# Held weight splits moved from GpSimd to VectorE, and the second token half of a skewed GEMM ordered behind the first

## The chip, the cores and the metric

The kernel runs on one core of a Trainium2 chip. The metric is device time in microseconds (us) of one launch; less is better. Three runs of the kernel before took 1042.84, 1040.69 and 1042.12 us, with a median of 1042.12 us.

## What is computed

One decoder block on 256 tokens of width 2048, all in float32. The part that matters here is the way from the mixer's output to the output of the block:

```python
mixed = jnp.concatenate([pool_out, attn_out], axis=-1) @ w_out[l]
h = h + rms_norm(mixed, post_mix_norm[l])

hn = rms_norm(h, pre_ffn_norm[l])
ff = (jax.nn.silu(hn @ w_gate[l]) * (hn @ w_up[l])) @ w_down[l]
h = h + rms_norm(ff, post_ffn_norm[l])
```

`w_out` is 2048 x 2048, `w_gate` and `w_up` are 2048 x 5632, and `w_down` is 5632 x 2048. Ahead of it stand a normalisation, the projection to queries, keys and values, a pooling mixer and differential attention.

## The kernel before

**How a product is made.** Every float32 weight tile is split into a high part and the rest: ScalarE copies the tile into a reduced format (the high part, L99), and another engine subtracts that from the original (the low part, L100). Activations are split the same way. A product is then three matmuls that add up in one PSUM bank: activation high by weight high (L135), activation low by weight high (L136), activation high by weight low (L137). So each 128-row step of the contraction, called a k-step below, costs three matmuls for each half of the tokens. The 256 tokens are two halves of 128, called t = 0 and t = 1, and each half has its own PSUM bank. Weights come in tiles of 128 x 1024 by DMA from SyncE's queue (L83), two k-steps to a tile, and are split tile by tile in `split` (L97).

**Two ways through a GEMM.** `gemm_a` (L141) takes the k-steps in order and does both token halves at each. `gemm_a_skew` (L149) does so too, except for a run of "held" k-steps: their split weights are kept, then all held k-steps are done for t = 0, and after that all of them for t = 1. If the last k-step is a held one, the function hands out the finished bank of t = 0 as soon as its matmuls are written, so that what follows for t = 0 can run beside the matmuls of t = 1.

Skewed GEMMs are used in three places:
- The last of four column blocks of `w_out` (`closing`, called at L609) holds its last 12 k-steps. What follows for each token half is the sum of squares (ScalarE, L536), the gain (VectorE, L540), a reciprocal root of a few tiny instructions (L190 to L205) and the addition to the residual in four column blocks (VectorE, L563, tile `xn`).
- The first column block of `w_gate` (L614) holds its first 12 k-steps, that is, six weight tiles. The first three go into ring buffers, the next three into the six `hold` buffers, which the held weights of `w_out` use before them.
- The last column block of `w_down` (`closing`, L850) holds its last 8 of 44 k-steps; behind it come the same steps as behind `w_out` (tile `x` instead of `xn`), and then the stores of the result (L848).

**Between `w_out` and `w_gate`.** The new residual has to be transposed for the gate GEMM: `h_parts` (L582) transposes a block of 128 tokens by 512 columns on TensorE (four matmuls by the identity, L586), and for each of its four k-steps ScalarE makes the high part (L592) and VectorE the low part (L593). The tables `H_OUT` and `H_GATE` say behind which held k-step each of these blocks is written: three blocks of t = 0 in the midst of the `w_out` matmuls of t = 1, the fourth behind the gate's first k-step, and the blocks of t = 1 behind the gate's held k-steps of t = 0 and, for the last block, of t = 1.

**What sets the order.** The order of instructions on each engine isn't the program's order. A planner runs the program against a cost model (L906) and puts next on an engine what it thinks can run first. `tc.issue_after(ins)` restrains it: what is written inside the block is placed behind `ins` on `ins`'s engine. `behind[0]` is such an instruction for the matmuls of `mm_a` (L134): it starts as nothing, and each call of `h_parts` sets it to its last transpose (L587). Nothing else sets it, so the matmuls of t = 1 aren't bound to follow those of t = 0 on that account, and in `w_down` the last setter is a transpose of long before.

**Who splits the held weights of the gate.** L615 gives `split` its buffers and its engine: the first three tiles are ring buffers with VectorE, the next three are hold buffers with GpSimd (`pool`). Those three subtractions are the only ones of the 128 x 1024 kind that GpSimd does.

Of the kernel before, what the change touches and what calls it, by code (L numbers as in the profile page):

```python
# [29 lines left out]
H_GATE = {(0, 0): (0, 3), (0, 7): (1, 0), (0, 9): (1, 1), (0, 11): (1, 2), (1, 2): (1, 3)}  # L30
RING = 3
# [14 lines left out]
def block_kernel(ctx: ExitStack, tc: tile.TileContext, x, xT, pos, cols, rows, lamv, invf, invcnt,  # L46
                 w_in, w_u, w_pool, w_out, w_g0, w_u0, w_gu, w_down, out):
    nc = tc.nc
    mm, act, dve, pool, sync = nc.tensor, nc.scalar, nc.vector, nc.gpsimd, nc.sync
# [10 lines left out]
    def nm(s):  # L60
        uid[0] += 1
        return f"{s}_{uid[0]}"
# [4 lines left out]
    def bank():  # L67
        return psum.tile([P, 512], F32, tag="mm", name=nm("mm"), bufs=4)
# [42 lines left out]
    def a_steps(srcs, order=None, held=range(0), parts=None):  # L111

        i = 0
        for s in order or range(len(srcs)):
            raws = [load(srcs[s], half) for half in range(2)]
            for half in range(2):
                by = parts(i) if i in held else ()
                if by != "halves":
                    hi, lo = split(raws[half], *by)
                for j in range(2):  # L120
                    c = slice(j * 512, (j + 1) * 512)
                    if by == "halves":
                        w = split(raws[half][:, c], lambda: (half_tile("wh"), half_tile("wl")))
                    else:
                        w = hi[:, c], lo[:, c]
                    yield i, 4 * s + 2 * half + j, *w
                    i += 1

    behind = [None]
    before_k = [lambda c, i: None]  # L130

    def mm_a(ps, a, t, k, wh, wl, first, last):

        with tc.issue_after(behind[0]) if behind[0] is not None else nullcontext():  # L134
            mm.matmul(ps[t][:, :], lhsT=a[0](k, t), rhs=wh, start=first, stop=False)  # L135
            mm.matmul(ps[t][:, :], lhsT=a[1](k, t), rhs=wh, start=False, stop=False)  # L136
            last_mm[0] = mm.matmul(ps[t][:, :], lhsT=a[0](k, t), rhs=wl, start=False, stop=last).ins  # L137

    last_mm = [None]
# [9 lines left out]
    def gemm_a_skew(srcs, a, nk, order, held_at, parts, hook):  # L149


        ps = [bank(), bank()]
        held = []
        for i, k, wh, wl in a_steps(srcs, order, held_at, parts):
            if i in held_at:
                held.append((i, k, wh, wl))
                if len(held) < len(held_at):
                    continue
                for t in range(2):
                    for n, (i, k, wh, wl) in enumerate(held):  # L160
                        mm_a(ps, a, t, k, wh, wl, i == 0, i == nk - 1)
                        hook(t, n)
                    if i == nk - 1:
                        yield t, ps[t]
            else:
                for t in range(2):
                    mm_a(ps, a, t, k, wh, wl, i == 0, i == nk - 1)
        if nk - 1 not in held_at:
            for t in range(2):
                yield t, ps[t]  # L170
# [358 lines left out]
    def closing(srcs_of, a, nk, gains, order, tail, parts, hook, done):  # L529
# [26 lines left out]
        for t, ps in gemm_a_skew(srcs_of(3), a, nk, order, range(nk - tail, nk), parts, hook):  # L556
            square(3, t, ps[:, :])
            v = variance(sst[:, t, 3:4], 1.0 / D, pre2[:, t:t + 1])
            gained(3, t, ps[:, :])
            rs = rsqrt(v)  # L560
            for c in range(4):
                for z in (slice(0, 256), slice(256, 512)) if c == 0 and t == 1 else (slice(0, 512),):
                    dve.scalar_tensor_tensor(h_c(c, t)[:, z], mg[c, t][:, z], rs, h_c(c, t)[:, z], ALU.mult, ALU.add)  # L563
                    done(c, t, z)
# [14 lines left out]
    hold_parts = lambda: (hold.tile([P, 1024], F32R, tag=f"h{z}", name=nm(f"h{z}"), bufs=HOLD // 2) for z in ("hi", "lo"))  # L579
    rstd3 = cp.tile([P, 2], F32, name="rstd3")  # L580

    def h_parts(t, c):  # L582

        tr = bank2() if c % 2 == 0 else psum2.tile([P, 512], F32, tag="hs", name=nm("hs"), bufs=2)
        for j in range(4):
            last = mm.transpose(tr[:, j * P:(j + 1) * P], xn[t][:, (4 * c + j) * P:(4 * c + j + 1) * P], ident)  # L586
        behind[0] = last.ins  # L587
        for j in range(4):
            k = 4 * c + j
            o = tr[:, j * P:(j + 1) * P]  # L590
            hi, lo = (z(k)[:, t * P:(t + 1) * P] for z in (hh_k, hl_k))
            behind_act[0] = act.activation(hi, o, AF.Copy, scale=g3(k)).ins  # L592
            dve.scalar_tensor_tensor(lo, o, g3(k), hi.bitcast(F32), ALU.mult, ALU.subtract)  # L593
# [3 lines left out]
    def h_stats(t):  # L597
        for c in range(4):
            j2 = cp.tile([P, 512], mybir.dt.bfloat16, tag="sqj", name=nm("sqj"), bufs=2)
            with tc.issue_after(behind_act[0]):  # L600
                act.activation(j2, h_c(c, t), AF.Square, accum_out=ss3[:, t, c:c + 1])
        ss3s = small([P, 1])
        dve.tensor_reduce(ss3s, ss3[:, t, :], AX.X, ALU.add)
        dve.tensor_copy(rstd3[:, t:t + 1], rsqrt(variance(ss3s, 1.0 / D)))

    def h_hook(at):
        return lambda t, n: h_parts(*at[t, n]) if (t, n) in at else None
# [4 lines left out]
    a_h = (lambda k, t: hh_k(k)[:, t * P:(t + 1) * P], lambda k, t: hl_k(k)[:, t * P:(t + 1) * P])  # L612
    sg = []
    for t, ps in gemm_a_skew([w_g0[i] for i in range(4)], a_h, NKD, None, range(HOLD),  # L614
                             lambda i: (ring_parts, dve) if i < 2 * RING else (hold_parts, pool), h_hook(H_GATE)):  # L615
        h_stats(t)
        sg.append(cp.tile([P, 512], F32, tag="gain", name=f"sg{t}", bufs=2))
        act.activation(sg[t], ps[:, :], AF.Silu, scale=rstd3[:, t:t + 1])
# [291 lines left out]
```

## Time and profile before

| | |
|---|---|
| Median of three runs | 1042.12 us |
| The profiled execution's own time | 1042.59 us |
| Its span from first to last instruction | 1040.8 us |
| Granted TensorE clock, mean over the span | 0.997 |
| TensorE matmul busy | 1018.6 us, 98% of the span |
| VectorE busy | 733.4 us, 70% |
| ScalarE busy | 538.8 us, 52% |
| GpSimd busy | 34.6 us, 3% |
| Chain that ended last | TensorE 85%, DMA 6%, VectorE 6% |

The times of the trace are counted from the span's start. A matmul's duration in the trace is a modelled one of 0.39 us, while matmuls that nothing holds up start 0.23 us apart; so a gap is best read from start to start. "Idle before" names what ended the idle time in front of an instruction. The chain of waits follows the work that ended last, back from the last instruction, and shows at each step what released it.

The stages that matter lie at these times: the held matmuls of `w_out` from 288.66 us, the matmuls of the first gate block from 309.13 us, ten rounds of gate and up blocks from 356.18 to 789 us, `w_down` to 1030.5 us, and the last steps and stores to 1040.8 us.

### The profile page before, as it was taken

What the parts mean: (1) busy time and instruction counts of PE and PEld (TensorE: products, weight loads), DVE (VectorE), ACT (ScalarE), POOL (GpSimd) and SP (SyncE); (2) the same over time, 40 slices, a digit from 0 to 9 for tenths busy, and PEclk for the clock granted to TensorE, in tenths of its full rate; (3) what the DMA queues carried; (4) which work ended last, traced back from release to release, by engine and by line L of the source; (5) the groups of instructions that cost most, each with busy time, mean ns of one, the idle gap of its engine ahead of it and who ended that gap; (6) DMA issues with size and microseconds to landing.
All of it is one profiled execution on the core that took longest, in us unless ns stands there. A gap on an engine that the chain in (4) does not pass through costs nothing.

```text
span 1040.8 us, 12565 instructions
## 1 busy us (share of the span) xinstructions
PE 1018.6 (98%) x4787; PEld 839.4 (81%) x4787; DVE 733.4 (70%) x847; ACT 538.8 (52%) x643; POOL 34.6 (3%) x57
## 2 busy tenths in 40 slices
PE   8999999999999999999999999999999999999996
PEld 5788888988877788888878878878888888888884
DVE  6648755875677978889798887888877664454444
ACT  6746545664547655454554545545555653343431
POOL 0003200210030000000000000000000000000000
PEclk9999999999999999999999999999999999999998
DMA  8853555456754556555655556645565575556542
GB/s 321 293 182 122 178 185 166 156 168 220 245 198 158 175 207 207 180 181 207 212 191 186 177 191 211 209 167 183 199 211 202 206 286 193 194 192 212 195 169 81
DMA packets 57517, 203.39 MB, mean 195 GB/s; under 512 B 6896, under 2 KB 7792, under 8 KB 56688
## 3 DMA queue, kind: packets, MB, share of 16 engines
q1 hardware_dynamic: 57168, 202.44, 56.8%
q8 instruction: 37, 0.61, 0.2%
q14 instruction: 24, 0.20, 0.1%
q10 hardware_dynamic: 288, 0.15, 0.0%
HBM read 198.37 MB, written 4.19 MB: 195 GB/s over the span
## 4 chain that ended last, share of the span: by engine, by line
PE 85%; DMA 6%; DVE 6%; issue 1%; SPq 1%; ACT 1%; DVEq 0%; ACTq 0%
PE mm L137 15%; PE mm L136 15%; PE mm L135 15%; PE mm L757 8%; PE mm L755 7%; PE mm L756 7%; DMA raw<-in_w_gu 4%; PE tr L757 2%; PE tr L756 2%; PE tr L755 2%; DVE wl L695 2%; PE mm L173 2%; PE mm L175 2%; PE mm L174 1%; PE m L755 1%; DVE xn L563 1%
## 5 line engine op out<-in xcount | busy, mean ns | idle before, releaser
L100 DVE TENSOR_TENSOR wl<-raw,wh 128x1024 fp32r<-128x1024 f32 x88 | 104.7, 1222 | 106.9 <-ACT wh L99 106.9
L100 DVE TENSOR_TENSOR wlo<-raw,whi 128x1024 fp32r<-128x1024 f32 x97 | 119.2, 1230 | 70.3 <-ACT whi L99 64.0
L99 ACT ACTIVATE wh<-raw 128x1024 fp32r<-128x1024 f32 x88 | 89.3, 1052 | 122.0 <-PE mm L136 117.3
L99 ACT ACTIVATE whi<-raw 128x1024 fp32r<-128x1024 f32 x97 | 102.1, 1057 | 78.0 <-PE mm L136 60.7
L136 PE MATMUL mm<-wh,gl 128*128 128x512 f32 x352 | 137.1, 390 | 0.0
L695 DVE TENSOR_TENSOR wl<-raw,wh 128x2048 fp32r<-128x2048 f32 x50 | 114.4, 2287 | 31.2 <-ACT wh L702 31.2
L135 PE MATMUL mm<-wh,gh 128*128 128x512 f32 x352 | 134.8, 389 | 0.0
L137 PE MATMUL mm<-wl,gh 128*128 128x512 f32 x352 | 130.7, 389 | 0.0
L755 PE MATMUL mm<-wh,h 128*128 128x512 f32 x330 | 128.6, 390 | 0.0
L756 PE MATMUL mm<-wh,h 128*128 128x512 f32 x330 | 128.6, 390 | 0.0
L757 PE MATMUL mm<-wl,h 128*128 128x512 f32 x330 | 115.6, 394 | 3.8 <-DVE wl L695 3.8
L702 ACT ACTIVATE wh<-raw 128x2048 fp32r<-128x2048 f32 x50 | 95.5, 1910 | 44.7 <-PE tr L756 39.8
L702 ACT ACTIVATE wh<-T 128x2048 fp32r<-128x2048 f32 x30 | 57.3, 1911 | 60.4 <-DVE T L706 55.4
L695 DVE TENSOR_TENSOR wl<-T,wh 128x2048 fp32r<-128x2048 f32 x30 | 68.6, 2287 | 23.1 <-ACT wh L702 23.1
L135 PE MATMUL mm<-whi,x 128*128 128x512 f32 x192 | 75.1, 395 | 3.5 <-ACT whi L279 2.7
L137 PEld LDWEIGHTS mm<-wl,gh 128*128 128x128 f32 x352 | 66.1, 188 | 13.7
L136 PEld LDWEIGHTS mm<-wh,gl 128*128 128x128 f32 x352 | 66.0, 188 | 13.8
L757 PEld LDWEIGHTS mm<-wl,h 128*128 128x128 f32 x330 | 61.9, 188 | 18.7 <-DVE wl L695 6.1
L135 PEld LDWEIGHTS mm<-wh,gh 128*128 128x128 f32 x352 | 66.0, 188 | 13.5
L136 PE MATMUL mm<-whi,x 128*128 128x512 f32 x192 | 74.6, 391 | 0.0
L756 PEld LDWEIGHTS mm<-wh,h 128*128 128x128 f32 x330 | 61.9, 188 | 13.0
L755 PEld LDWEIGHTS mm<-wh,h 128*128 128x128 f32 x330 | 62.0, 188 | 12.6
(243 smaller groups left out, 1910.6 us busy)
## 6 DMA issues: line engine op xcount, KB each, us to landing
raw<-in_w_gu SPq DMA_DIRECT2D x160, 512.0 KB, 4.5
raw<-in_w_down SPq DMA_DIRECT2D x88, 512.0 KB, 4.1
raw<-in_w_in SPq DMA_DIRECT2D x46, 512.0 KB, 3.7
raw<-in_w_out SPq DMA_DIRECT2D x32, 512.0 KB, 4.0
raw<-in_w_u SPq DMA_DIRECT2D x24, 512.0 KB, 3.6
raw<-in_w_g SPq DMA_DIRECT2D x8, 512.0 KB, 5.9
xn<-in_x SPq DMA_DIRECT2D x2, 1024.0 KB, 9.1
gain<-in_rows SPq DMA_DIRECT2D x8, 256.0 KB, 4.9
```

Of the source, the lines that this page charges most:

```text
L99: last_split[0] = act.activation(hi, raw, AF.Copy).ins
L100: (by or dve).tensor_tensor(lo, raw, hi.bitcast(F32), ALU.subtract)
L135: mm.matmul(ps[t][:, :], lhsT=a[0](k, t), rhs=wh, start=first, stop=False)
L136: mm.matmul(ps[t][:, :], lhsT=a[1](k, t), rhs=wh, start=False, stop=False)
L137: last_mm[0] = mm.matmul(ps[t][:, :], lhsT=a[0](k, t), rhs=wl, start=False, stop=last).ins
L173: mm.matmul(o, lhsT=wh, rhs=xh, start=st, stop=False)
L175: mm.matmul(o, lhsT=wl, rhs=xh, start=False, stop=sp)
L695: last_low[0] = dve.tensor_tensor(res, x, hi.bitcast(F32), ALU.subtract).ins
L702: act.activation(res, x, AF.Copy)
L755: mm.matmul(o, lhsT=a[0], rhs=wh, start=first, stop=False)
L756: mm.matmul(o, lhsT=a[1], rhs=wh, start=False, stop=False)
L757: mm.matmul(o, lhsT=a[0], rhs=wl, start=False, stop=left[i] == 0)
```

## The change

Two edits, each of a line. In `gemm_a_skew`, after the held matmuls of a token half, `behind[0]` is set to the last of them. So the matmuls of t = 1 are placed behind all held ones of t = 0, and whatever `mm_a` writes later is placed behind the last held one of t = 1. It holds in all three skewed GEMMs. It also replaces what `h_parts` had set inside the loop. In the gate's call, the engine is taken out of the pair: all six held tiles are split by VectorE, which is the default of `split`; the buffers are the same.

```diff
@@ -160,6 +160,7 @@
                     for n, (i, k, wh, wl) in enumerate(held):
                         mm_a(ps, a, t, k, wh, wl, i == 0, i == nk - 1)
                         hook(t, n)
+                    behind[0] = last_mm[0]
                     if i == nk - 1:
                         yield t, ps[t]
             else:
@@ -612,7 +613,7 @@
     a_h = (lambda k, t: hh_k(k)[:, t * P:(t + 1) * P], lambda k, t: hl_k(k)[:, t * P:(t + 1) * P])
     sg = []
     for t, ps in gemm_a_skew([w_g0[i] for i in range(4)], a_h, NKD, None, range(HOLD),
-                             lambda i: (ring_parts, dve) if i < 2 * RING else (hold_parts, pool), h_hook(H_GATE)):
+                             lambda i: (ring_parts if i < 2 * RING else hold_parts,), h_hook(H_GATE)):
         h_stats(t)
```

## The prediction

> **What bounds the kernel now.** I read the page's header first, then the chain of waits between the end of `w_out` and the ten rounds, then the timelines of each engine there and behind the last matmul.
>
> ```profile
> span 1040.8 us, 12565 instructions
> PE 1018.6 (98%) x4787; PEld 839.4 (81%) x4787; DVE 733.4 (70%) x847; ACT 538.8 (52%) x643; POOL 34.6 (3%) x57
> ```
>
> TensorE is the bound for nearly the whole span, so a change that adds or drops no matmul can win only where TensorE stands still, or behind its last matmul. The chain shows where:
>
> ```profile
> 299.30 9.25 DVE xn L563 x4
> ...
> 314.62 2.77 DVE xn L563 x5
> ...
> 317.72 0.50 PE mm L136
> ```
>
> It runs on TensorE before this and after it. In between VectorE holds it. Four residual additions of t = 0 take 9.25 us; the same four blocks of t = 1 (five instructions, one block being halved) take 2.77. Beside the slow ones stands the only other thing that differs:
>
> ```profile
> L563 DVE SCALAR_TENSOR_TENSOR xn<-mg,tiny,xn x2: 2874/2934/2993, 299.3 to 302.2; 128x512 f32<-128x512 f32 x2
> ...
> 307.90:308.60 0.70, 0.65 (x1) 1.00 0.00 0
> L100 POOL TENSOR_TENSOR hlo<-raw,hhi x3: 2400/2836/2837, 299.3 to 304.5; 128x1024 fp32r<-128x1024 f32 x3
> ```
>
> The first row has VectorE's first two additions, of 2.99 and 2.87 us (the three times are the least, the median and the most, in ns). The second is a stretch in which only the fourth runs, for 0.65 us, so about 2.7 us are left for the third: 9.25 - 2.99 - 2.87 - 0.65. The third row has GpSimd's three splits, which begin at 299.3 and end at 304.5 + 2.84 = 307.3. So three additions each last about one GpSimd split, and the fourth, after GpSimd is done, 0.65 us. That is taking turns: each waits until the other's whole instruction is over.
>
> The Trainium skill, SBUF — State Buffer, section Who interferes with whom, states this: a VectorE instruction with both inputs in SBUF and a GpSimd instruction that reads SBUF use one port in turn, and the later one is blocked for the other's whole length. The 2.87 us beside the 0.65 us agree with it.
>
> **What the first edit is worth.** TensorE waits for these additions three times, since the transposes of `h_parts` read `xn`:
>
> ```profile
> 301.35 0.39 PE L137 MATMUL mm<-hlo,mh 128*128 128x512 f32 x1
> 302.35 0.66 PE L586 MATMUL tr<-ident,xn 128*128 128x128 f32 x4 [0.61 <-DVE xn L563]
> ...
> 304.00 0.40 PE L137 MATMUL mm<-hlo,mh 128*128 128x512 f32 x1
> 305.14 0.65 PE L586 MATMUL hs<-ident,xn 128*128 128x128 f32 x4 [0.75 <-DVE xn L563]
> ...
> 306.80 0.40 PE L137 MATMUL mm<-hlo,mh 128*128 128x512 f32 x1
> 307.94 0.66 PE L586 MATMUL tr<-ident,xn 128*128 128x128 f32 x4 [0.74 <-DVE xn L563]
> ...
> 309.58 0.39 PE L137 MATMUL mm<-wlo,h 128*128 128x512 f32 x1
> 309.81 0.60 PE L586 MATMUL hs<-ident,xn 128*128 128x128 f32 x4
> 310.17 0.48 PE L135 MATMUL mm<-whi,h 128*128 128x512 f32 x1
> ...
> 315.07 0.83 PE L586 MATMUL tr<-ident,xn 128*128 128x128 f32 x4
> 315.66 0.48 PE L135 MATMUL mm<-hhi,h 128*128 128x512 f32 x1
> ...
> 316.67 0.60 PE L586 MATMUL hs<-ident,xn 128*128 128x128 f32 x4
> 317.72 0.50 PE L136 MATMUL mm<-hhi,h 128*128 128x512 f32 x1 [0.45 <-DVE h L593]
> ```
>
> I count from start to start. A block of transposes that nobody holds up starts 0.23 us behind the matmul before it (309.58 to 309.81), and the next matmul 0.36 us after that. The three held-up ones start 1.00, 1.14 and 1.14 us behind: too late by 0.77 + 0.91 + 0.91 = 2.59 us. At 315.07 and 316.67 the next matmul comes after 0.59 and 1.05 us: too late by 0.23 + 0.69 = 0.92 us.
>
> Without GpSimd the four additions take about 2.8 us and end near 302.1. The three splits come to VectorE instead:
>
> ```profile
> L100 DVE TENSOR_TENSOR wlo<-raw,whi 128x1024 fp32r<-128x1024 f32 x97 | 119.2, 1230 | 70.3 <-ACT whi L99 64.0
> 300.87 1.06 ACT L99 ACTIVATE hhi<-raw 128x1024 fp32r<-128x1024 f32 x1 [0.30 <-PE mm L136]
> 313.70 0.39 PE L135 MATMUL mm<-hhi,h 128*128 128x512 f32 x1
> ```
>
> Three times 1.23 is 3.69 us. Even with all of them ahead of the `h` splits, VectorE comes to those at 299.3 + 2.8 + 3.7 = 305.8 rather than at 299.30 + 9.25 = 308.55, so it gains 2.7 us while it does the more work. If one split stands ahead of each addition, they end at 301.2, 303.2 and 305.1, and TensorE, unheld, asks for them at 301.6, 303.4 and 305.2: still no stall. Only if all three splits stood ahead of the first addition (the third can't start before its high part is made at 300.87 + 1.06 = 301.9) would that addition end at 301.9 + 1.23 + 0.7 = 303.9, and TensorE would wait 2.3 of its 2.6 us again. So this term is between 0.3 and 2.6; I take 2.59, since the additions are ready at 299.3 and the second and third splits aren't. The matmuls with the moved weights start at 313.70, so by 311 in the new run, and the splits are done by 306 or so: nobody waits for them. SyncE's loads wait for the raw tiles that these splits free, which comes sooner than GpSimd's 307.3.
>
> The 0.92 us hang on t = 1's additions at 314.6. Their chain starts with ScalarE's sum of squares:
>
> ```profile
> 308.90 0.39 PE L137 MATMUL mm<-hlo,mh 128*128 128x512 f32 x1
> 311.73 0.59 ACT L536 ACTIVATE sqj<-mm 128x512 bf16<-128x512 f32 x1
> ```
>
> The bank of t = 1 is ready at 308.90 + 0.39 = 309.29, but ScalarE gets to it 2.44 us later, since it is still at the `h` parts that VectorE held up. With those done sooner it can start at once, so relative to TensorE the additions come up to 2.4 us sooner, and the 0.92 us go too. Bounds: 0 (VectorE, fuller by 3.7 us, hands the delay on) and 1.2 (some matmuls up to 319.6 also start late by tenths). I take 0.92. First edit: 2.59 + 0.92 = 3.5 us, with bounds 0.3 and 3.8.
>
> Does it survive to the end? Behind 317.72 the waits view has these two rows for TensorE, and no other:
>
> ```profile
> PE mm L757 <- DVE wl L695: 3.8, 4, 1.2
> PE mm L755 <- ACT rh L702: 0.5, 1, 0.5
> ```
>
> The second is one wait at the start of the ten rounds, the first four waits in them (total, times, longest). The loads and splits that end them wait in their turn for buffers that TensorE frees, so a start that is 3.5 us sooner moves all of it. I put the passing on at no cost, with the rounds' order as a rival below.
>
> **What the second edit is worth.** In the gate the new order forbids filling t = 1's held steps with later k-steps; the `h` parts those need should come over 2 us sooner by the first edit, so I price that at zero (a stall there could cost some tenths). The other two places show in the matmuls, in ScalarE's sums of squares and in what VectorE does behind them:
>
> ```profile
> 297.07 0.60 ACT L536 ACTIVATE sqj<-mm 128x512 bf16<-128x512 f32 x1 [5.97 <-PE mm L137]
> ...
> 1019.44 0.39 PE L135 MATMUL mm<-wh,gh 128*128 128x512 f32 x1
> ...
> 1028.48 0.60 ACT L536 ACTIVATE sqj<-mm 128x512 bf16<-128x512 f32 x1 [7.06 <-PE mm L137]
> 1029.20 0.21 DVE L190 TENSOR_SCALAR tiny<-sst,tiny 128x1 f32<-128x1 f32 x1 [6.33 <-ACT sqj L536]
> 1030.10 0.39 PE L137 MATMUL mm<-wl,gh 128*128 128x512 f32 x1
> 1030.52 0.60 ACT L536 ACTIVATE sqj<-mm 128x512 bf16<-128x512 f32 x1 [0.87 <-PE mm L137]
> 1033.36 0.21 DVE L190 TENSOR_SCALAR tiny<-sst,tiny 128x1 f32<-128x1 f32 x1
> ```
>
> In `w_out` t = 0's sum starts at 297.07, 12 us ahead of the end of t = 1's bank at 309.29: the halves are in order already, and the edit is worth nothing there. In `w_down` the planner mixed them. The last matmul ends at 1030.10 + 0.39 = 1030.49. The 48 held ones start at 1019.44, so they are (1030.10 - 1019.44) / 47 = 0.227 us apart. With the halves in order, t = 0 ends 24 of them sooner, at 1025.05; now its sum of squares starts only at 1028.48. VectorE's steps for t = 0 run from 1029.20 to 1033.36, and only then does it take up t = 1, whose sum of squares started at 1030.52. In order, t = 0's 4.16 us begin at about 1025.8 and end at 1030.0, before t = 1 needs VectorE: 0.72 us behind 1030.52 (the step from 1028.48 to 1029.20), at 1031.24 instead of 1033.36. That is 2.12 us, and what follows stays as long as it is. It needs t = 0's last weights in time:
>
> ```profile
> 1019.41 2.01 ACT L99 ACTIVATE wh<-raw 128x1024 fp32r<-128x1024 f32 x2 [3.43 <-PE mm L136]
> 1020.51 2.36 DVE L100 TENSOR_TENSOR wl<-raw,wh 128x1024 fp32r<-128x1024 f32 x2 [3.08 <-ACT wh L99]
> ```
>
> In order, the fifth k-step's come 12 matmuls later, at 1022.2, the seventh's at 1023.5, each low part 0.45 us after that; the splits are done at 1021.7 and 1022.9. A margin of 0.9 us or more, so no stall. I keep 1.6 to 2.4 as bounds for small shifts.
>
> **Sum.** 3.5 + 2.1 = 5.6 us. The profiled execution's own 1042.59 becomes 1037.0; it is 0.47 above the median of 1042.12, which becomes 1036.5.
>
> **The rivals.** *The order in the rounds changes (slower).* The planner lays the program out anew, and the rounds depend on how transfers and splits fall. Four waits of 3.8 us in all, the longest 1.2, hold TensorE up in ten rounds; from start to start a wait is 0.16 us longer (0.77 against 0.61 above), so 4.4 us in all and 1.4 at most. If all ten rounds took the worst layout, that is 14 us, 9.6 more: 1036.5 + 9.6 = 1046.1. It decides against the change once more than four further rounds wait (4 x 1.4 = 5.6). For it: rounds of the same code now come out differently. Against: the planner sees about the same inputs there. The same thing the other way, no waiting round, would give 1036.5 - 4.4 = 1032.1.
>
> *VectorE becomes the bound.*
>
> ```profile
> 297.00:309.00 12.00, 9.90 (x48) 7.43 (x48) 10.87 (x11) 4.50 (x8) 8.00 (x3) 1.00 0.15 54
> 309.00:321.00 12.00, 11.55 (x58) 8.76 (x57) 9.54 (x31) 6.75 (x24) 0.00 (x0) 1.00 0.74 264
> ```
>
> The third busy figure is VectorE's: 10.87 + 9.54 = 20.4 of 24 us. If the 9.25 us of additions were real work, 3.69 more would make 24.1 and push t = 1's additions and all behind them by up to 3.7: 1042.1 + 3.7 - 2.1 = 1043.7, slower than before by less than can be told. The Trainium skill, Perfetto Trace Analysis, section Optimizing Scalar/DVE Operations, speaks for this rival: where VectorE is saturated, handing work to GpSimd may pay (it adds that the shared port may spoil it). The 0.65 us of the fourth addition says that 6.5 of the 9.25 us are waiting, so I give it little.
>
> *Only the end is gained.* The planner sets the splits ahead of the additions: 0.3 of the first edit and 2.1 of the second, 1042.1 - 2.4 = 1039.7.
>
> *The second edit does nothing,* since the planner's mixing came from elsewhere: 1042.1 - 3.5 = 1038.6. The edit forbids the mixing by name, so this is the least likely.
>
> **Chances.** Forecast 0.62 (1035.9 to 1038.0: 2.5 to 3.8 us by the first edit, 1.6 to 2.4 by the second); only the end 0.14; rounds better 0.08, rounds worse 0.08; VectorE bound 0.05; second edit void 0.03. The range runs from 1033.5 (half of the better rounds) to 1039.8. About 0.2%, 2.1 us, is what a measurement of this kernel can tell from no change: faster means below 1040.0. The forecast, most of the end-only case, the better rounds and the void edit lie there: 0.84. Slower (above 1044.2) takes most of the worse rounds: 0.06. The rest, 0.10, is the same.
>
> **What would show it.** The four additions of t = 0 should take about 0.7 us each with no GpSimd instruction beside them; the idle time ahead of the transposes that VectorE ended (0.61, 0.75, 0.74) should be gone, and the gate's first matmul should come 2.6 us sooner; t = 1's sum of squares in `w_out` should start within 0.5 us of its bank's end. At the end, t = 0's sum of squares should start 5.4 us ahead of t = 1's, and some 8.2 us, not 10.3, should lie between the last matmul and the span's end. I am wrong if the additions stay near 2.9 us, if a wait for a low part `hlo` appears, or if the rounds' length changes by over 0.5 us each.

## The result and the profile after

The changed kernel took 1055.98 us (median of four runs, 1053.40 to 1057.19); the kernel before took 1042.44 us beside it (1040.69 to 1042.84). The ratio is 1.013, with a 95% interval of 1.0114 to 1.0147: slower, where 1036.5 us had been forecast. The profiled execution took 1056.83 us. In the changed kernel every line from L164 on has a number one greater than before.

First the page's header and the shares of the chain.

```profile
span 1055.0 us, 12573 instructions
PE 1024.1 (97%) x4787; PEld 841.9 (80%) x4787; DVE 730.0 (69%) x850; ACT 539.7 (51%) x643; POOL 26.6 (3%) x54
...
PE 80%; DVE 7%; DMA 7%; issue 3%; ACT 2%; SPq 1%; DVEq 0%; ACTq 0%
```

The matmuls are as many as before. TensorE's share of the chain fell from 85 to 80%, so it stood still more. To see where, I cut each span at four marks: the first held matmul of `w_out` (`hhi` by `mh`), the first product of the rounds (`rh` by `h`), the first of `w_down` (`wh` by `gh`) and the last L135 matmul.

| us | middle | ten rounds | `w_down` | end |
|---|---|---|---|---|
| before | 67.5 | 433.3 | 240.1 | 11.1 |
| after | 65.7 | 452.1 | 240.2 | 9.0 |

Both places that the change touches became shorter, by 1.9 and 2.1 us (taken before rounding). The ten rounds, in which it changes no line, became 18.8 us longer.

**The middle,** from the timeline of the changed kernel:

```profile
299.81 2.73 DVE L564 SCALAR_TENSOR_TENSOR xn<-mg,tiny,xn 128x512 f32<-128x512 f32 x4
301.01 0.60 PE L587 MATMUL tr<-ident,xn 128*128 128x128 f32 x4
...
305.80 0.39 PE L135 MATMUL mm<-whi,h 128*128 128x512 f32 x1
...
306.06 0.60 ACT L537 ACTIVATE sqj<-mm 128x512 bf16<-128x512 f32 x1 [0.58 <-PE mm L137]
...
312.06 0.50 PE L136 MATMUL mm<-whi,h 128*128 128x512 f32 x1 [1.27 <-DVE h L594]
```

The four additions of t = 0 take 2.73 us instead of 9.25, and the transposes have no idle time noted. The gate's first matmul comes 17.7 us behind the first mark (305.80 - 288.08) instead of 20.5 (309.13 - 288.66). The sum of squares of t = 1 waits for TensorE alone. The last row is a wait of a kind that the kernel before has once, with 0.45 us (at 317.72): TensorE waits 1.27 us for a low part of `h`.

**The end,** from the timelines of TensorE, ScalarE and VectorE:

```profile
1041.43 0.60 ACT L537 ACTIVATE sqj<-mm 128x512 bf16<-128x512 f32 x1 [3.65 <-PE mm L137]
...
1046.44 0.39 PE L137 MATMUL mm<-wl,gh 128*128 128x512 f32 x1
1046.87 0.60 ACT L537 ACTIVATE sqj<-mm 128x512 bf16<-128x512 f32 x1 [4.27 <-PE mm L137]
1047.59 0.21 DVE L191 TENSOR_SCALAR tiny<-sst,tiny 128x1 f32<-128x1 f32 x1 [1.20 <-ACT sqj L537]
```

The sum of squares of t = 0 stands 5.44 us ahead of that of t = 1, VectorE takes t = 1 up 0.72 us behind it, and 8.2 us lie between the last matmul's end (1046.83) and the span's.

**The rounds.** TensorE's waits behind 318 us in the changed kernel (total, times, longest):

```profile
PE mm L756 <- ACT wh L703: 5.2, 4, 1.7
PE m L756 <- ACT gT L677: 5.0, 9, 0.7
PE mm L756 <- ACT rh L703: 3.9, 5, 1.8
PE mm L758 <- DVE wl L696: 3.5, 4, 1.3
```

Before there were 4.3 us in 5 waits; now there are 17.6 us in 22. That is 13.3 us more, and 17 more times the 0.16 us that a wait is longer from start to start, 2.7. The windows of 10 us show the rest (behind the window and its length stand the busy times of TensorE's matmuls, its weight loads, VectorE, ScalarE and GpSimd, with their instructions in brackets, then the granted clock, the DMA share and GB/s):

```profile
500.00:510.00 10.00, 7.93 (x32) 5.87 (x31) 6.46 (x6) 4.05 (x3) 0.00 (x0) 0.94 0.38 134
510.00:520.00 10.00, 10.00 (x41) 8.13 (x40) 4.99 (x3) 3.74 (x3) 0.00 (x0) 0.89 0.76 268
580.00:590.00 10.00, 6.74 (x29) 4.76 (x29) 8.22 (x8) 6.28 (x7) 0.00 (x0) 1.00 0.10 29
670.00:680.00 10.00, 7.26 (x26) 5.15 (x24) 8.07 (x8) 4.99 (x5) 0.00 (x0) 0.83 0.02 5
```

The clock is below 0.995 in three windows of the rounds, which costs at most (0.06 + 0.11 + 0.17) x 10 = 3.4 us. In all that makes 13.3 + 2.7 + 3.4 = 19.4, against 18.8 measured. In two of these windows the DMA share is 0.10 and 0.02: the loads have stopped. ScalarE's timeline shows what it was doing at 580:

```profile
571.90 1.92 ACT L703 ACTIVATE wh<-T 128x2048 fp32r<-128x2048 f32 x1 [4.25 <-PE tr L757]
580.93 1.49 ACT L703 ACTIVATE rh<-raw 128x1536 fp32r<-128x1536 f32 x1 [7.11 <-DMA raw<-in_w_gu]
582.32 0.71 ACT L796 ACTIVATE sg<-sg,rstd 128x512 f32<-128x512 f32 x1
582.94 1.89 ACT L703 ACTIVATE wh<-raw 128x2048 fp32r<-128x2048 f32 x1
```

and the waits of SyncE's queue from 556 to 592 us, what that did to the loads:

```profile
SPq L691 <- DVE wl L696: 23.2, 3, 13.5
```

A round works on eight blocks of weights, numbered 0 to 7, each of 1 MB, each loaded by SyncE into one of three `raw` tiles. ScalarE waits 7.11 us for block 2 (`rh`), while block 1 (`wh`, at 582.94), loaded before it, stands behind it in ScalarE's queue. Until block 1 is copied and VectorE has its low part, its tile isn't free, and SyncE waits 13.5 us with the next load. Then TensorE waits for both.

The order in which the planner put the instructions explains it. In the kernel before, ScalarE copies block 1 and then block 2 in every round, and SyncE loads the blocks in their order. In the changed kernel block 2's copy stands ahead of block 1's in rounds 2 to 10, and in rounds 3, 6, 8 and 10 SyncE loads block 3 ahead of block 2. The trace shows what the second thing adds: ScalarE waits 5.9, 7.1, 7.3 and 5.7 us for block 2's load in those four rounds and at most 0.8 us in the other five.

That isn't the whole loss. Added up over windows of 10 us, some 10.7 us of TensorE's idle time lie in the stretches 440 to 450, 580 to 590, 670 to 690 and 760 to 780 us, which belong to the four rounds. But 3.3 us lie between 490 and 510 us, in round 4, whose loads come in their order. There the queue that blocks is VectorE's:

```profile
498.85 1.92 ACT L703 ACTIVATE wh<-raw 128x2048 fp32r<-128x2048 f32 x1 [0.52 <-PE tr L757]
...
504.20 1.23 DVE L707 TENSOR_TENSOR T<-raw 128x1024 f32<-128x1024 f32 x1 [3.54 <-DMA raw<-in_w_gu]
505.34 2.28 DVE L696 TENSOR_TENSOR wl<-raw,wh 128x2048 fp32r<-128x2048 f32 x1
...
507.68 0.50 PE L758 MATMUL mm<-wl,h 128*128 128x512 f32 x1 [1.25 <-DVE wl L696]
```

The high part made at 498.85 is done at 500.77, but VectorE makes its low part (block 3's) only at 505.34, because a sum for block 5 (tile `T`) stands ahead of it and waits for block 5's load. So VectorE's order turned too, and the planner moved three queues, not two.

### The profile page after: what moved, and what is told of

Same layout as the page of the kernel before. It is cut to its first block, busy times and chain, and to the rows that moved or that the text cites. A ratio compares the mean times of both kernels' runs of the same rounds, so it can differ in the third digit from the quotient of the medians.

```text
span 1055.0 us, 12573 instructions
## 1 busy us (share of the span) xinstructions
PE 1024.1 (97%) x4787; PEld 841.9 (80%) x4787; DVE 730.0 (69%) x850; ACT 539.7 (51%) x643; POOL 26.6 (3%) x54
## 4 chain that ended last, share of the span: by engine, by line
PE 80%; DVE 7%; DMA 7%; issue 3%; ACT 2%; SPq 1%; DVEq 0%; ACTq 0%
PE mm L137 15%; PE mm L136 15%; PE mm L135 15%; PE mm L758 6%; PE mm L756 6%; PE mm L757 6%; DMA raw<-in_w_gu 5%; DVE wl L696 3%; PE tr L758 2%; PE tr L757 2%; PE tr L756 2%; PE mm L174 2%; PE mm L176 1%; PE mm L175 1%; DVE T L707 1%
## 5 line engine op out<-in xcount | busy, mean ns | idle before, releaser
L756 PE MATMUL mm<-wh,h 128*128 128x512 f32 x330 | 130.1, 394 | 5.2 <-ACT wh L703 5.2
L135 PE MATMUL mm<-wh,gh 128*128 128x512 f32 x352 | 134.8, 389 | 0.0
L757 PE MATMUL mm<-wh,h 128*128 128x512 f32 x330 | 129.8, 393 | 0.0
L756 PEld LDWEIGHTS mm<-wh,h 128*128 128x128 f32 x330 | 62.5, 189 | 19.8 <-ACT wh L703 7.0
L135 PE MATMUL mm<-whi,x 128*128 128x512 f32 x192 | 75.2, 395 | 2.0 <-ACT whi L280 1.3
L135 PEld LDWEIGHTS mm<-wh,gh 128*128 128x128 f32 x352 | 66.0, 188 | 13.8
```

Of the source, the lines that this page charges most:

```text
L756: mm.matmul(o, lhsT=a[0], rhs=wh, start=first, stop=False)
L757: mm.matmul(o, lhsT=a[1], rhs=wh, start=False, stop=False)
```

## The experiments

The first theory, **A**, is that this other order is the whole loss, and that it comes only of both edits together, through the planner. Rivals: **B**, the earlier start makes the rounds' transfers fall worse, whatever the order; **C**, the ordering in the gate is itself to blame. The stages of all kernels, and their times against the kernel before, run beside them (its medians were 1040.89, 1041.46, 1042.11 and 1041.61 us in the four groups; the stage times are those of one profiled execution each). Edits are shown against the changed kernel where nothing else is said.

| kernel | middle | rounds | end | span | median | ratio, 95% interval |
|---|---|---|---|---|---|---|
| split_only | 66.5 | 432.1 | 11.1 | 1040.2 | 1040.83 | 0.9997, 0.9985 to 1.0009 |
| behind_only | 67.4 | 431.1 | 9.0 | 1035.6 | 1039.32 | 0.9977, 0.9964 to 0.9990 |
| split_tail | 66.5 | 432.7 | 9.0 | 1037.0 | 1038.54 | 0.9977, 0.9964 to 0.9990 |
| after_one_edge | 65.6 | 432.5 | 9.0 | 1036.3 | 1038.05 | 0.9969, 0.9956 to 0.9982 |
| after_loads_in_order | 65.7 | 435.9 | 9.0 | 1038.6 | 1041.34 | 1.0000, 0.9990 to 1.0009 |
| pool_reads | 72.2 | 431.4 | 9.0 | 1041.7 | 1043.83 | 1.0024, 1.0014 to 1.0035 |
| low_parts_behind_h3 | 65.5 | 435.1 | 9.0 | 1040.3 | 1039.26 | 0.9976, 0.9966 to 0.9986 |
| low_parts_behind_h11 | 66.5 | 433.5 | 9.0 | 1039.2 | 1040.96 | 0.9997, 0.9988 to 1.0007 |
| swapped_loads_only | 65.7 | 430.1 | 9.0 | 1035.6 | 1036.82 | 0.9941, 0.9922 to 0.9959 |
| split_and_gate | 65.6 | 453.1 | 11.1 | 1058.8 | 1063.36 | 1.0198, 1.0161 to 1.0234 |
| swapped_in_nine_rounds | 65.6 | 427.6 | 9.0 | 1032.0 | 1033.82 | 0.9927, 0.9914 to 0.9941 |
| one_edge_again | 65.6 | 432.7 | 9.0 | 1038.2 | 1038.52 | 0.9968, 0.9958 to 0.9978 |

`w_down` is 240.1 us in each. What lies ahead of the first mark varies by about 1.5 us up or down from run to run, so I compare stages, not spans. The rounds themselves vary: with block 1 copied ahead of block 2 and the loads in order, they lie between 431.1 and 435.1 us in the kernel before and eight of these. So the ratios decide where stages differ by less than that.

**split_only: the first edit alone.**

```diff
-                    behind[0] = last_mm[0]
```

> The first edit alone: VectorE makes all six held low parts of the gate, and nothing is ordered behind anything. Theory A (the loss of the whole change is the planner's other order in the ten rounds, which neither edit has by itself): the planner's order in the rounds is that of before here, so the rounds take what they took before (433 us from first to last product) and start some 2.5 us sooner, as in the profile after; about 1039 to 1040 us. Theory B (the rounds suffer because they start sooner, in whatever order, since loads and splits then fall otherwise): the rounds take 445 us or more, 1050 us or more in all.

The rounds took 432.1 us: without the second edit nothing is lost in them. The middle gained 1.0 us instead of 3.5, and the time is that of the kernel before within 0.15%, 0.8 us above the range that A gave.

**behind_only: the second edit alone.**

```diff
-                             lambda i: (ring_parts if i < 2 * RING else hold_parts,), h_hook(H_GATE)):
+                             lambda i: (ring_parts, dve) if i < 2 * RING else (hold_parts, pool), h_hook(H_GATE)):
```

> The second edit alone, in all three skewed GEMMs; GpSimd keeps its three splits. Theory A: order in the rounds as before, start as before, and 2.1 us gained behind the last matmul: 1040.3 us. Theory B: the rounds start as before, so 1040.3 too. Theory C (the new order of the gate's held matmuls costs by itself, with the first edit or without): TensorE stalls in the gate or the rounds, 1050 us or more.

The rounds took 431.1 us and the end 9.0 instead of 11.1. So neither edit has the loss by itself.

**split_tail: both, without the ordering in `w_out` and the gate.** (Only `w_down` has `NF` k-steps.)

```diff
-                    behind[0] = last_mm[0]
+                    if nk == NF: behind[0] = last_mm[0]
```

> The first edit, and the second one in w_down alone; in w_out and in the gate the matmuls of the second half are as free as before. Theory A: the planner keeps the order of before in the rounds, both gains are there, 2.5 to 3.5 us ahead of the rounds and 2.1 behind the last matmul: 1036.8 to 1037.8 us. Theory B: the rounds start as early as in the changed kernel, so they are as slow: about 1054 us.

Rounds of 432.7 us after a start that is 1.0 us sooner than before (66.5 against 67.5 us): this speaks against B. But the changed kernel's start is 1.9 us sooner, and only the next run has that. The time is 0.7 us above A's range.

**after_one_edge: the changed kernel with block 2's copy placed behind block 1's.**

```diff
-    def high(x, tag):
+    def high(x, tag, after=None):
...
-        act.activation(res, x, AF.Copy)
+        with (tc.issue_after(after) if after else nullcontext()): made[tag] = act.activation(res, x, AF.Copy).ins
...
-        rh = high(raw[:, 1:4], "rh")
+        rh = high(raw[:, 1:4], "rh", made["wh"] if j == 2 else None)
```

> The whole change, with one thing more: in each round ScalarE's high part of block 2 (its three kept columns) is placed behind its high part of block 1. In the changed kernel block 2 comes first in most rounds, and ScalarE waits for its load with block 1 behind it. With the edge the planner also returns to the loads' order of before. Theory A: the rounds take about 433 us again and the whole gain appears: 1036.5 to 1038.5 us. Theories B and C: the edge changes little, since the early start and the gate's order are as in the changed kernel: 1050 us or more.

One edge, which the planner honours by going back to the old order of the loads and, from round 3 on, of VectorE too, takes 19.6 us off the rounds, with both edits and the early start (65.6 us) in place. B and C fall and A holds: 1038.05 us, better than both kernels.

**split_and_gate: both, with the ordering in the gate alone.** (`w_out` and `w_down` hold their last k-step, so this leaves both out.)

```diff
-                    behind[0] = last_mm[0]
+                    if nk - 1 not in held_at: behind[0] = last_mm[0]
```

> The change without its part in w_down: VectorE splits the held weights, and the gate's tail is ordered, but w_down's tail is left as it was. Its order in the rounds is that of the changed kernel on ScalarE and SyncE. If the other order in the rounds is the whole loss, and comes of these two together: middle 65.6 us, rounds 452 us, end 11.2 us, so the time is 2.2 us over the changed kernel's, 1056 to 1059 us. If w_down's ordering had a part in the loss: under 1053 us.

The middle, the rounds and the end are as expected, and so is the other order: the parts in `w_out` and `w_down` have no share in the loss. The median lies 4 us above the range. Its four runs are spread from 1059.33 to 1066.19 us; the profiled one took 1060.59. The two longest had a granted clock of 0.990 against 0.996 in the profiled one; 0.006 of 1066 us is 6.4 us by this estimate, about what they are longer. But the shortest had 0.993, so the clock doesn't explain the spread by itself.

**after_loads_in_order: which of the two orders costs?** The changed kernel with the loads put straight and ScalarE's order left as it is.

```diff
-            latest[0] = sync.dma_start(raw[:, 2 * half:2 * half + 2], s).ins
+            with (tc.issue_after(latest[0]) if j == 3 else nullcontext()): latest[0] = sync.dma_start(raw[:, 2 * half:2 * half + 2], s).ins
```

> The changed kernel with one more edge: in each of the ten rounds, SyncE's load for block 3 is issued behind the load for block 2. In the changed kernel two things differ in the rounds from the kernel before: ScalarE copies block 2's weights (rh) ahead of block 1's (wh), and in four of the rounds SyncE loads block 3 ahead of block 2. This kernel puts the loads straight and leaves ScalarE's order as it is. Theory A1 (ScalarE's order is the price: the copy that waits for a load stands in front of one whose data have landed, so a buffer isn't freed and the loads stop): the ten rounds stay above 440 us against 433.3 us before, and the time stays at 1045 to 1056 us. Theory A2 (the loads that come in the wrong order are the price): the rounds return to 431 to 434 us, and the time to 1037 to 1040 us.

A1, which was my reading of the trace, falls: ScalarE's order alone costs 3.4 us in the rounds (435.9 against 432.5; the ratios, 1.0000 against 0.9969, say 3.2 us), not the bulk. A2 comes near, with 431 to 434 us. TensorE's waits behind 318 us:

```profile
PE m L756 <- ACT gT L677: 2.4, 9, 0.5
PE mm L758 <- DVE wl L696: 0.8, 5, 0.2
PE mm L756 <- ACT wh L703: 0.5, 1, 0.5
PE mm L756 <- ACT rh L703: 0.3, 1, 0.3
```

The copy still stands in front, and ScalarE waits 3.8 to 4.8 us for block 2 in rounds 3 to 10. But block 2, loaded ahead of block 3, lands soon enough that this seldom reaches TensorE: the longest wait is 0.5 us, where the changed kernel has 1.8. So is it the loads' order by itself? That was the next run.

**swapped_loads_only: the loads swapped in rounds 3, 6, 8 and 10, block 2's copy behind block 1's.** (The edge of after_one_edge is in it too and isn't shown again.)

```diff
+    early = {}
+    def fetch(src, j, raw, after=None):
...
-    def blocks(src, j):
+    def blocks(src, j, swap=False):
+        if j in early:
+            return early.pop(j)
         raw = part("raw", 4, F32, 3)
+        if swap and j == 2:
+            early[3] = part("raw", 4, F32, 3)
+            fetch(src, 3, early[3])
+            fetch(src, 2, raw, latest[0])
...
-        raw = blocks(w_gu[c - 1], j)
+        raw = blocks(w_gu[c - 1], j, c in (3, 6, 8, 10))
```

> The changed kernel with ScalarE's copies of block 2 behind those of block 1 in each round (as after_one_edge, rounds 432.5 us, 1038.05 us), and with the loads of block 3 put ahead of block 2 in rounds 3, 6, 8 and 10, as the changed kernel has them. It fills the fourth field of a table of two by two: the changed kernel has both orders bent (rounds 452.1 us), after_loads_in_order has ScalarE's order bent alone (435.9 us). In the four rounds the planner here puts the copy of block 2 behind that of block 3 as well, so ScalarE takes the blocks in the order in which they land. Theory H (the price is a copy that waits at the head of ScalarE's queue for a load that lands late, while a copy whose data have landed stands behind it; the later load alone costs little): the rounds take 432 to 437 us, the time is 1037.5 to 1042 us, and ScalarE's waits of 7 us for a load are not there. Theory S (the swapped loads are the price, whatever ScalarE's order): the rounds take 445 to 450 us, the time is 1050 to 1056 us.

One thing in that text is wrong: in the program as built, block 2's copy stands behind block 1's and one copy out of PSUM, but still ahead of block 3's. The rounds took 430.1 us, so S falls; H's range, 432 to 437 us, was too high as well. The four fields are (ratios to the kernel before in brackets):

| rounds, us | loads in order | block 3 loaded ahead of 2 in four rounds |
|---|---|---|
| block 1 copied ahead of 2 | 432.5 (0.9969) | 430.1 (0.9941) |
| block 2 copied ahead of 1 | 435.9 (1.0000) | 452.1 (1.0130) |

Neither order costs much alone; in its first row the second column even gains, though 2.4 us are within the scatter of the rounds. Together they cost 19.6 us. That is theory H, with one condition more than it had: in this run too ScalarE waits 2.6 to 3.8 us for block 2 in the four rounds, with block 3's data landed 2.4 to 3.6 us earlier and its copy standing behind, and nothing is lost. In the changed kernel the copy behind is block 1's, whose tile the next load needs. So the late load hurts where it holds up the tile that the next load needs.

One thing limits the table: the planner lays out each of these kernels anew, and VectorE's order goes with it. In after_loads_in_order block 3's low part stands ahead of block 5's sum in round 4 again. So it is shown that the turned order as a whole is the loss and that neither of the two orders makes it alone; how the 19.6 us divide between ScalarE's queue in the four rounds and VectorE's in round 4 is not.

**swapped_in_nine_rounds, and one_edge_again beside it.** The 2.4 us that the swap gained asked for more of it.

```diff
-        raw = blocks(w_gu[c - 1], j, c in (3, 6, 8, 10))
+        raw = blocks(w_gu[c - 1], j, c > 1)
```

> As swapped_loads_only, with the loads of block 3 ahead of block 2 in rounds 2 to 10 instead of rounds 3, 6, 8 and 10. Theory F (a load should be issued in the order in which its buffer comes free; block 0 of a round is worked off ahead of block 7 of the round before, so block 3's buffer is free some 2.3 us before block 2's, and SyncE in the straight order lets it lie): the four swaps took the rounds from 432.5 to 430.1 us, 0.6 us each, so nine take them to 427.1 us, and the time to 1033 to 1035 us. Rival G (the 2.4 us are scatter between runs, or the other five rounds have nothing to gain): the rounds stay at 429.5 to 432.5 us, the time within 1 us of after_one_edge of the same call, or of 1036.8 us.

> The kernel of after_one_edge again, for a comparison on one chip with the run before: rounds 432.5 us within 1, time 1037 to 1039 us, 0.996 to 0.998 of the kernel before.

The rounds fell to 427.6 us, where F expected 427.1 and G 429.5 or more; one_edge_again had 432.7. TensorE's waits from 318 to 790 us, of one_edge_again and then of swapped_in_nine_rounds, whose lines are twelve higher:

```profile
PE mm L758 <- DVE wl L696: 3.5, 4, 1.1
PE mm L756 <- ACT rh L703: 0.2, 1, 0.2
```

```profile
PE mm L770 <- DVE wl L708: 0.8, 2, 0.5
PE mm L768 <- ACT rh L715: 0.2, 1, 0.2
```

So this is the fastest version, 0.9927 of the kernel before (0.9914 to 0.9941). F's reason doesn't stand, though. In the sixth round SyncE issues the two loads 0.9 us apart in either order (567.15 and 568.06 in after_one_edge, 566.73 and 567.64 here), so no tile lay free for 2.3 us. What differs there is VectorE's order. First after_one_edge, then swapped_in_nine_rounds:

```profile
573.49 1.22 DVE L707 TENSOR_TENSOR T<-raw 128x1024 f32<-128x1024 f32 x1
574.62 0.75 DVE L665 SCALAR_TENSOR_TENSOR gg<-u,rstd,sg 128x512 f32<-128x512 f32 x1
575.28 2.29 DVE L696 TENSOR_TENSOR wl<-raw,wh 128x2048 fp32r<-128x2048 f32 x1
```

```profile
572.43 0.74 DVE L665 SCALAR_TENSOR_TENSOR gg<-u,rstd,sg 128x512 f32<-128x512 f32 x1
573.09 2.28 DVE L708 TENSOR_TENSOR wl<-raw,wh 128x2048 fp32r<-128x2048 f32 x1
...
576.12 1.23 DVE L719 TENSOR_TENSOR T<-raw 128x1024 f32<-128x1024 f32 x1
```

With the swap, the sum `T` of block 2 comes behind block 1's low part instead of ahead of it, so block 1's tile is free sooner: the next load starts at 575.40 instead of 577.60. In the programs as built VectorE has this order in the swapped rounds and in no other. That it is what the swap is worth was read from one round and not tried by itself.

**pool_reads: are the additions slow because GpSimd reads beside them?** split_tail, with GpSimd's three subtractions made as well, into a tile that nobody reads; the edit is shown against split_tail.

```diff
-        last_split[0] = act.activation(hi, raw, AF.Copy).ins
+        last_split[0] = act.activation(hi, raw, AF.Copy).ins; also and also(raw, hi)
...
+    idle = hold.tile([P, 1024], F32, tag='idle', name='idle', bufs=1)
+    beside = lambda raw, hi: pool.tensor_tensor(idle, raw, hi.bitcast(F32), ALU.subtract)
...
-                             lambda i: (ring_parts if i < 2 * RING else hold_parts,), h_hook(H_GATE)):
+                             lambda i: (ring_parts,) if i < 2 * RING else (hold_parts, None, beside), h_hook(H_GATE)):
```

> Both parts of the change but without the ordering in the gate (as split_tail, 1038.5 us), and beside that GpSimd again makes the three held subtractions from the same tiles, into a tile that nobody reads: added work, whose result isn't used. VectorE still makes the low parts that the products use. Theory L (GpSimd's large pass slows VectorE's additions while both run): the additions of t=0 that lie beside a GpSimd subtraction take about 2.9 us each again instead of 0.7, the waits of up to 2.6 us at the transposes come back in part, the stretch from the first held w_out product to the first product of the rounds grows from 66.6 us to 67.5 to 70, and the time is 1039 to 1042 us. Rival M (the additions were slow in the kernel before for another reason, such as their place in VectorE's order or the banks that they read): the additions stay at 0.7 us each, the stretch at 66.6 us within 0.5, the time at 1038 to 1039 us.

The two groups of instructions (least, median and most in ns):

```profile
L564 DVE SCALAR_TENSOR_TENSOR xn<-mg,tiny,xn x4: 741/2868/2871, 300.6 to 309.0; 128x512 f32<-128x512 f32 x4
...
L614 POOL TENSOR_TENSOR idle<-raw,hhi x3: 2717/2718/3410, 299.5 to 305.8; 128x1024 f32<-128x1024 f32 x3
```

Three additions take 2.87 us again and the one behind GpSimd's last 0.74: L holds, M falls. The middle, 72.2 us, went past the range and past the 67.5 us of the kernel before: VectorE now has the turns to wait for and the splits to do, and the first low part of `h` comes at 311.92 instead of 305.30. That is the prediction's rival of a full VectorE, seen here where the waiting had not gone.

**low_parts_behind_h3 and low_parts_behind_h11: can the new wait in the middle be ordered away?** after_one_edge, with the gate's held low parts placed behind a low part of `h`, that of k-step 3 (shown) or that of k-step 11.

```diff
-        (by or dve).tensor_tensor(lo, raw, hi.bitcast(F32), ALU.subtract)
+        with (tc.issue_after(late) if late else nullcontext()): dve.tensor_tensor(lo, raw, hi.bitcast(F32), ALU.subtract)
...
-                             lambda i: (ring_parts if i < 2 * RING else hold_parts,), h_hook(H_GATE)):
+                             lambda i: (ring_parts,) if i < 2 * RING else (hold_parts, lows[0, 3]), h_hook(H_GATE)):
```

> The changed kernel with ScalarE's order in the rounds put right (as after_one_edge, 1038.05 us), and the three held low parts on VectorE ordered behind the low part of h of k-step 3 of t=0, so that VectorE does the additions and the first low parts of h before them. Theory D (the gain in the middle fell short of 3.5 us because VectorE works off 3.6 us of held low parts ahead of what TensorE waits for, and the 1.3 us wait for a low part of h behind t=1's additions follows from that): the wait goes or falls under 0.5 us, the stretch from the first held w_out product to the rounds falls from 65.6 to 64.2 to 65.0 us, the time is 1036.5 to 1037.5 us. Rival E (VectorE's total work in this stretch is the limit, so what is put later waits later): another wait of about 1 us appears, for a held low part or a later low part of h, the stretch stays within 0.5 us of 65.6, the time within 0.7 us of 1038.

> As the run before, with the held low parts behind the low part of h of k-step 11 of t=0, so behind t=1's additions as well. Theory D: no wait of over 0.5 us for a low part of h is left, the stretch is 64.2 to 65.0 us, unless the gate's first product with a held low part now waits for it; that product is some 8 us later than the low parts of h, so that this costs under 1 us. Rival E: the stretch stays at 65.6 us or grows to 67, with a wait for a held low part (hlo) of 1 us or more.

TensorE's waits in the middle, of after_one_edge, then of the one and the other:

```profile
PE mm L136 <- DVE h L594: 1.3, 1, 1.3
```

```profile
PE mm L136 <- DVE h L594: 1.6, 1, 1.6
```

```profile
PE tr L587 <- DVE h L594: 1.9, 1, 1.9
PE mm L137 <- DVE hlo L100: 0.5, 1, 0.5
```

The wait moves and doesn't shrink, the middle stays at 65.5 us or grows to 66.5, and the ratios, 0.9976 and 0.9997, are no better than after_one_edge's 0.9969: E holds and D falls, though the first one's time came out above both ranges. In this stretch VectorE's work is the limit. (The 435.1 us of rounds in low_parts_behind_h3 belong to the slowest of its twelve executions, 1042.11 us.)

## Why the prediction was wrong

**The step that failed** is "I put the passing on at no cost". The stall times, the buffers and the transfers did pass on a start that came 1.9 us sooner, where the rounds had the old order (after_one_edge: 432.5 us). In the changed kernel the order didn't stay. "The planner sees about the same inputs there" was the ground for a chance of 0.08, and the planner's choice turned out to hang on such small differences that each edit alone leaves it and both together turn it. What in the cost model tips it was not looked into and stays open. The price was short as well: 9.6 us, if all ten rounds took the worst layout that the trace of before had. The trace of before had no round with this layout, so its worst wait (1.4 us) was no bound for it; it cost 18.8 us. The prediction had named a change of over 0.5 us in each round as a sign of being wrong; it was 1.9 us in the mean.

**The first edit, 3.5 us,** gave about 1.9 with the gate's ordering and 1.0 without. The term of 2.59 us was right: the gate's first matmul came 2.75 us sooner, the additions took 0.7 us each, and pool_reads shows the cause. But the waits at the transposes are not the whole of it. In behind_only VectorE's first addition comes ahead of GpSimd's first split and takes 0.75 us, and the gate's first matmul comes 2.2 us sooner with GpSimd still at work; yet the middle is 67.4 us, since TensorE then waits for the first low part of `h`:

```profile
PE mm L136 <- DVE h L594: 1.9, 2, 1.5
```

VectorE comes to that low part 19.8 us behind the first mark in the kernel before, 19.7 us in behind_only and 16.7 us in the changed kernel. That VectorE is free sooner is what the first edit is worth. The term of 0.92 us was wrong, even with t = 1's sum of squares starting on time: t = 1's five additions now stand on VectorE ahead of a low part of `h` that TensorE waits for, at 312.06, 1.42 us late from start to start (1.65 instead of 0.23). 2.75 + 0.92 - 1.42 is 2.25, so 0.4 us aren't accounted for. Its bound of 0, a fuller VectorE that hands the delay on, was the better value and still too high.

**The second edit** was right in `w_out` (nothing) and at the end (2.1 us measured, 2.12 forecast, with the 5.4 and 8.2 us as announced). In the gate I had put zero. It is worth 0.9 us beside the first edit: split_only and split_tail have a second wait in the middle, here in split_tail,

```profile
PE hs L587 <- DVE h L594: 0.7, 1, 0.7
```

a transpose in `w_gate` behind a low part of `h`, which is gone in all kernels that have the gate's ordering. Its other effect there was to turn the rounds.

**The rivals.** The sign was that of the rounds' order, whose sum of 1046.1 us was 10 us too low. A full VectorE cost part of the middle, not the 3.7 us. Had the order stayed, the time would have been that of after_one_edge, 0.9969 of before, so about 1039 instead of 1036.5.

## What to carry to other kernels

Where a planner sets the order, an edit can turn the order of a loop far behind it. So compare the order on every engine's queue ahead of pricing the edit, and pin an order that matters by an edge. Look at what stands behind an instruction that waits for a load at the head of its queue: if it is the one that frees the tile of the next load, the loads stop, and two shifts that cost little apart can make that together. The order in which the loads land is not the rule: in the fastest kernel here block 2's copy waits up to 3.7 us with block 3's data already there. When VectorE is rid of waiting, look at what stands behind its new work; here ordering moved that wait and took nothing off it.

## What was not expected of the hardware

A stall can cost TensorE more than its own length. Windows of the changed kernel, in the columns as above (the granted clock is the third from the end):

```profile
505.32:508.73 3.41, 1.78 (x7) 1.18 (x8) 3.41 (x4) 2.12 (x2) 0.00 (x0) 1.00 0.05 11
508.73:512.14 3.41, 3.41 (x10) 2.63 (x9) 3.41 (x3) 0.00 (x0) 0.00 (x0) 0.50 0.81 294
...
580.41:583.82 3.41, 1.90 (x8) 0.93 (x6) 2.85 (x3) 2.89 (x3) 0.00 (x0) 1.00 0.00 0
...
672.57:675.98 3.41, 1.57 (x6) 0.99 (x7) 3.41 (x5) 3.41 (x4) 0.00 (x0) 1.00 0.01 2
675.98:679.39 3.41, 3.41 (x9) 2.63 (x10) 3.41 (x4) 0.90 (x2) 0.00 (x0) 0.50 0.00 0
```

TensorE was busy for 1.78 and for 1.57 of 3.41 us, and right behind each of these windows it ran at half clock for 3.41 us, losing 1.7 us. These are the two places where the clock fell in the rounds of the changed kernel. From 581 to 585 us TensorE was busy for 1.43 of 4 us and kept its clock. The grid explains it: the second fall comes 675.98 - 508.73 = 167.25 us behind the first, 49 times 3.413 us, and on a grid of such steps the 4 us lie across two windows, with 1.90 and 2.35 busy us. In the rounds of the changed kernel the two windows of this grid with the least busy time are those that the half clock follows. No limit comes out of it: in low_parts_behind_h11 a window with 1.52 busy us (312.43 to 315.84) was followed by the full clock.

The Trainium skill, TensorE: Matmul & The Clock Gate, section Part 1: The HAM clock gate, has a clock that is halved after an idle window of about 3.4 us, counted in windows that run freely. The half clock, the 3.41 us and the grid agree; idle the windows were not, but busy for 52% and 46%. In the rounds of the kernel before, after_one_edge, after_loads_in_order and swapped_in_nine_rounds no window of 10 us is below 0.995.
